# Neighbourhood attention in two steps per block: scores and softmax, then transposes and value products

## The chip, the cores and the metric

The kernel runs on one core of one Trainium2 chip. The metric is the device time in microseconds. A core has a matrix engine (TensorE, PE in the profile; PEld is its loading of stationary operands), a vector engine (VectorE, DVE), an activation engine (ScalarE, ACT), GpSimd (POOL) and SyncE (SP), which here issues the transfers from memory. Each engine works through its own queue in the order in which the kernel was laid out. Matmuls write to PSUM, an accumulator memory that this kernel uses as eight banks of 128 x 512 float32; all other tiles lie in SBUF.

## The reference

A backbone of two layers over 512 latent tokens and 256 context tokens of width 1024, in float32. Every layer has a mixing part, whose three head groups share one input and one output projection, and then a SwiGLU feed-forward part. The mixing part has a gated MLP (A), neighbourhood attention (B) and a bidirectional mLSTM (C). The change concerns B. It has 6 heads of 64 channels; the 512 latent tokens form a grid of 8 rows by 64 columns, and each query sees all 8 rows in a window of 16 columns, clipped at the edges, with a relative bias, and all 256 context tokens:

```python
s_win = jnp.einsum('bhqd,bhqkd->bhqk', q_blk, k_win).astype(jnp.float32) * scale + bias.astype(jnp.float32)
s_ctx = jnp.einsum('bhqd,bhkd->bhqk', q_blk, k_ctx).astype(jnp.float32) * scale
p = jax.nn.softmax(jnp.concatenate([s_win, s_ctx], axis=-1), axis=-1).astype(v.dtype)
return (jnp.einsum('bhqk,bhqkd->bhqd', p[..., :win], v_win)
        + jnp.einsum('bhqk,bhkd->bhqd', p[..., win:], v_ctx))
```

In the first layer the context tokens also attend to the context. The last layer gives no context output.

## The kernel before

Everything is laid out feature by token. A dense product (`dense`, line 137) splits its float32 operands into a high and a low part and makes three matmuls per 128 x 128 weight tile; the weights are loaded by `wload` (line 122) on SP's queue and split by ScalarE (`whi`, line 128) and VectorE (`wlo`, line 129). These products are `dps` in the profile.

The mixing part of a layer is written as Python generators: `do_B(p)` and `do_C(p)` for three pairs of heads each (p = 0, 1, 2), `do_A`, `do_o` (the output gate of C), `do_Cv` (v), `do_Crows` (r), and `do_mods` (m, modulation weights, layer 0 only). A string per layer, `ORDERS[l]` (line 31), says which generator takes its next step and how many, so `B0:3` is three steps of the first head pair. This gives the order in which the code issues instructions. A planner then draws up the queue of each engine from it, when the kernel is built: it takes instructions by their place in that order and by durations that it assumes, so a later instruction that it thinks ready goes ahead of an earlier one that it thinks is not. It also gives tiles their buffers. `after` (line 132) ties one instruction behind another on the same engine. Neither the planner nor its durations are part of the change.

`do_B(p)` (line 483) first makes keys, values and queries of two heads (`bk`, `bv`, `bq`), transposes the values (`bvt`) and loads two bias tiles. Then it goes through attention blocks of 128 queries, one generator step each: three blocks of 16 grid columns each (m = 0, 1, 2) with 256 window keys and 256 context keys; one block of the two edges of the grid, twice 64 queries with 128 window keys each, and 256 context keys; and in layer 0 two blocks of 128 context queries with 256 context keys. That is 18 blocks in layer 0 and 12 in layer 1.

One block is `attend` (line 532). Both heads' scores go to two PSUM tiles (`bsps`). Then for each head in turn: VectorE adds the bias and finds the negated maximum (`nm`), ScalarE takes the exponential and its sum (`prob`, line 564), VectorE inverts the sum and multiplies (line 566), TensorE transposes the probabilities in pieces of 128 x 128 (`ptps`, line 569) and ScalarE copies them to SBUF (`probT`, line 571). Then the value products of both heads run into `bops`, and VectorE copies these to the result `bo`. The PSUM tiles of a block come from the pool `mx`, with four banks, which serves the transposes and products of A, C and the normalisations as well; `dense` takes most of its tiles from the pool `mm`, with three banks. `prob`, `probT` and other working tiles share a pool of seven SBUF buffers, and `bk`, `bv`, `bq`, `bvt` share another seven with the gate, the A group and, afterwards, the residual x, which is loaded back on SP's queue (lines 1056 to 1061).

After the mixing steps the results of A, C and B are split into high and low parts (`put_y`, line 1034) for the output projection.

Of the kernel before, what the change touches and what calls it, by code (L numbers as in the profile page):

```python
# [38 lines left out]
)  # L39
FWD, BWD = [0, 1, 2, 3, 4, 5], [1, 0, 5, 4, 3, 2]  # L40

# [2 lines left out]
def tile_backbone(ctx: ExitStack, tc: tile.TileContext, A, out):  # L44
    nc = tc.nc
    te, ve, ac, gp, sp = nc.tensor, nc.vector, nc.scalar, nc.gpsimd, nc.sync
# [12 lines left out]
    mx = ctx.enter_context(tc.tile_pool(name="mx", bufs=4, space=PSUM))  # L59
# [32 lines left out]
    def pst(pool, name="ps"):  # L92
        return pool.tile([128, 512], F32, tag="ps", name=name)
# [4 lines left out]
    def small(n, name="sm"):  # L98
        return st.tile([128, n], F32, tag="sm%d" % n, name=name)
# [4 lines left out]
    def zat(name, dt=F32):  # L104
        return za.tile([128, 768], dt, tag="z", name=name)
# [208 lines left out]
    for toks in ((2, 3, 4, 5), (0, 1)):  # L314
# [13 lines left out]
        n = len(toks)  # L328
        o = 256 if n == 4 else 0
# [89 lines left out]
    wlast, prev = None, None  # L419
    for k in range(KD):  # L420
# [10 lines left out]
        for stream in (0, 1):  # L431
            prev = norm1_k(0, h_next, x, stream, k)
# [10 lines left out]
    for l in range(2):  # L443
        last = l == 1
# [33 lines left out]
                    te.transpose(out=ps[:, i * 128:(i + 1) * 128], in_=src(c), identity=ident)  # L478
                dst(g, ps)

        bq_t = []

        def do_B(p):
            ku, vu, qu = zat("bk"), zat("bv"), zat("bq")
# [11 lines left out]
            for wi_, (c0, u, is_q) in enumerate(((896, ku, False), (1280, vu, False), (512, qu, True))):  # L496
# [7 lines left out]
                if is_q:  # L504
                    ac.activation(
                        out=u[:, 256:640].rearrange("p (b r i) -> p r b i", b=3, r=8),
                        in_=p3[:, :, 8:56].rearrange("p r (b i) -> p r b i", b=3), func=AF.Copy, scale=sc)
                    for e, cc in enumerate((0, 56)):
                        ve.tensor_scalar(
                            out=u[:, 640 + 64 * e:704 + 64 * e].rearrange("p (r i) -> p r i", r=8),  # L510
                            in0=p3[:, :, cc:cc + 8], scalar1=sc, scalar2=None, op0=ALU.mult)
                else:
                    ac.activation(
                        out=u[:, 256:768].rearrange("p (m r c) -> p r m c", m=4, r=8),
                        in_=p3.rearrange("p r (m c) -> p r m c", m=4), func=AF.Copy)
                if len(parts) > 1:
                    ve.tensor_scalar(out=u[:, 0:256], in0=pp[1], scalar1=sc, scalar2=None, op0=ALU.mult)
            yield
            vt = zat("bvt")
            transposes(  # L520
                lambda g, ps: ac.activation(
                    out=vt[:, g[0] * 128:(g[-1] + 1) * 128], in_=ps[:, 0:len(g) * 128], func=AF.Copy),
                lambda c: vu[:, c * 128:(c + 1) * 128], range(6))
            bias = []
            for j in range(2):
                b = wk.tile([128, 390], F32, tag="bias", name="bias", bufs=2)
                i = sp.dma_start(out=b[:, 0:384], in_=A["bias"][l, 2 * p + j])
# [1 line left out]
                    after(i, start_end)  # L529
                bias.append(b)  # L530

            def attend(q0, segs, L, btile, ops, ocol):
                n = L + 256
                spss = [pst(mx, "bsps") for _ in range(2)]
                jss = [slice(64 * j, 64 * j + 64) for j in range(2)]
                order = [None]

                def chained(*args, **kw):
                    m = te.matmul(*args, **kw)  # L539
                    if order[0] is not None:  # L540
                        after(m, order[0])
                    order[0] = m

                if L == 128:
                    for e in range(2):
                        for sps, js in zip(spss, jss):
                            chained(
                                out=sps[64 * e:64 * e + 64, 0:128], lhsT=qu[js, q0 + 64 * e:q0 + 64 * e + 64],
                                rhs=ku[js, 256 + 384 * e:384 + 384 * e])
                elif L:  # L550
                    for sps, js in zip(spss, jss):
                        chained(
                            out=sps[:, 0:256], lhsT=qu[js, q0:q0 + 128], rhs=ku[js, segs[0] * 128:segs[0] * 128 + 256])
                for sps, js in zip(spss, jss):
                    chained(out=sps[:, L:n], lhsT=qu[js, q0:q0 + 128], rhs=ku[js, 0:256])
                pTs = []
                for j, sps in enumerate(spss):
                    if L:
                        ve.tensor_tensor(out=sps[:, 0:L], in0=sps[:, 0:L], in1=btile[j], op=ALU.add)  # L559
                    nm = small(1, "nm")  # L560
                    ve.tensor_reduce(out=nm, in_=sps[:, 0:n], axis=AX.X, op=ALU.max, negate=True)  # L561
                    pt = wkt("prob")
                    sm_ = small(1, "sum")
                    ac.activation(out=pt[:, 0:n], in_=sps[:, 0:n], func=AF.Exp, bias=nm, accum_out=sm_)  # L564
                    ve.reciprocal(out=sm_, in_=sm_)
                    ve.tensor_scalar(out=pt[:, 0:n], in0=pt[:, 0:n], scalar1=sm_, scalar2=None, op0=ALU.mult)  # L566
                    tps = pst(mx, "ptps")
                    for i in range(n // 128):
                        te.transpose(out=tps[:, i * 128:(i + 1) * 128], in_=pt[:, i * 128:(i + 1) * 128], identity=ident)  # L569
                    pT = wkt("probT")  # L570
                    ac.activation(out=pT[:, 0:n], in_=tps[:, 0:n], func=AF.Copy)
                    pTs.append(pT)
                order[0] = None
                if L == 128:
                    for e in range(2):
                        for i, c in enumerate((2 + 3 * e, 0, 1)):
                            for j, js in ((1, jss[1]), (0, jss[0])):
                                chained(
                                    out=ops[js, ocol + 64 * e:ocol + 64 * e + 64], lhsT=vt[:, c * 128 + 64 * j:c * 128 + 64 * j + 64],
                                    rhs=pTs[j][:, i * 128 + 64 * e:i * 128 + 64 * e + 64], start=(i == 0), stop=(i == 2))  # L580
                else:
                    tl = list(segs) + [0, 1]
                    for i, c in enumerate(tl):
                        for j, js in ((1, jss[1]), (0, jss[0])):
                            chained(
                                out=ops[js, ocol:ocol + 128], lhsT=vt[:, c * 128 + 64 * j:c * 128 + 64 * j + 64],
                                rhs=pTs[j][:, i * 128:(i + 1) * 128], start=(i == 0), stop=(i == len(tl) - 1))

            yield
            res = zct("bo")  # L590
            r3 = res[:, 256:768].rearrange("p (r c) -> p r c", c=64)
            for m in range(3):
                ops = pst(mx, "bops")
                attend(256 + 128 * m, (2 + m, 3 + m), 256, [b[:, 0:256] for b in bias], ops, 0)
                ve.tensor_copy(
                    out=r3[:, :, 8 + 16 * m:24 + 16 * m], in_=ops[:, 0:128].rearrange("p (r i) -> p r i", r=8))
                yield
            ops = pst(mx, "bops")
            attend(640, (), 128, [b[:, 256:384] for b in bias], ops, 0)
            for e, cc in enumerate((0, 56)):  # L600
                ve.tensor_copy(
                    out=r3[:, :, cc:cc + 8], in_=ops[:, 64 * e:64 * e + 64].rearrange("p (r i) -> p r i", r=8))
            yield
            if not last:
                for i in range(2):
                    ops = pst(mx, "bops")
                    attend(128 * i, (), 0, None, ops, 0)
                    ve.tensor_copy(out=res[:, 128 * i:128 * i + 128], in_=ops[:, 0:128])
                    yield
            bq_t.append(res)  # L610

        v65 = [zct("v65").rearrange("p (c h d) -> p c h d", c=2, h=6) for _ in range(3)]
        for t in v65:
# [389 lines left out]
            gens["B%d" % p], gens["C%d" % p] = do_B(p), do_C(p)  # L1003
        for stp in ORDERS[l].split():
            nm, _, cnt = stp.partition(":")
            for _ in range(int(cnt or 99)):
                if next(gens[nm], 0) == 0:
                    break
        for gen in gens.values():
            for _ in gen:  # L1010
                pass
        while fill:
            fill.pop(0)()

# [112 lines left out]
        for pi, (f0, nf) in enumerate(FF_PIECES):  # L1127
# [5 lines left out]
            for fi in range(nf):  # L1133
                f = f0 + fi
# [14 lines left out]
                for pgi, pui, g in zip(pg, pu_, gs):  # L1149
                    o, T = g[1] + (256 if g[0] == "l" else 0), g[2]  # L1150
# [128 lines left out]
```

## Time and profile before

| what | value |
|---|---|
| device time, median of 3 runs | 1732.04 us (1729.26 to 1732.41) |
| the profiled execution's own time | 1729.28 us |
| its span, from first to last instruction | 1726.4 us |
| TensorE busy | 1660.5 us, 96% |
| VectorE busy | 936.3 us, 54% |
| ScalarE busy | 615.3 us, 36% |
| GpSimd busy | 148.2 us, 9% |
| mean granted TensorE clock | 0.984 |

How to read it: the profile is one execution; times in it count from the first instruction. A row of a group gives the line, the engine, the operation, the tile written and the tiles read, then the count, busy time, mean length in ns, and the idle time of the engine directly before, with what ended it. A row of the waits reads "engine tile line <- engine tile line that ended the wait: us in total, times, longest". The granted clock is a share of full speed. Each share is a mean over stages with different limits.

### The profile page before, as it was taken

What the parts mean: (1) busy time and instruction counts of PE and PEld (TensorE: products, weight loads), DVE (VectorE), ACT (ScalarE), POOL (GpSimd) and SP (SyncE); (2) the same over time, 40 slices, a digit from 0 to 9 for tenths busy, and PEclk for the clock granted to TensorE, in tenths of its full rate; (3) what the DMA queues carried; (4) which work ended last, traced back from release to release, by engine and by line L of the source; (5) the groups of instructions that cost most, each with busy time, mean ns of one, the idle gap of its engine ahead of it and who ended that gap; (6) DMA issues with size and microseconds to landing.
All of it is one profiled execution on the core that took longest, in us unless ns stands there. A gap on an engine that the chain in (4) does not pass through costs nothing.

```text
span 1726.4 us, 26247 instructions
## 1 busy us (share of the span) xinstructions
PE 1660.5 (96%) x10784; PEld 1416.0 (82%) x10784; DVE 936.3 (54%) x1697; ACT 615.3 (36%) x1126; POOL 148.2 (9%) x157
## 2 busy tenths in 40 slices
PE   7998999889999999999999999989989999999998
PEld 5886777768888888888888889777869988888888
DVE  4589787635475555344443355585675633333335
ACT  4444344633332211222112244534654522222225
POOL 0000112122200000000000020012033000000000
PEclk9999999979999999999999999989999999999999
DMA  8742313213244434334333233210213322222222
GB/s 290 250 151 70 123 59 102 74 35 102 62 136 132 123 122 135 125 126 128 122 122 104 74 117 105 71 56 28 86 62 117 105 98 98 93 94 94 98 82 95
DMA packets 57143, 184.11 MB, mean 107 GB/s; under 512 B 6720, under 2 KB 8384, under 8 KB 56896
## 3 DMA queue, kind: packets, MB, share of 16 engines
q1 hardware_dynamic: 57024, 182.45, 32.7%
q8 instruction: 84, 1.38, 0.3%
q14 instruction: 35, 0.29, 0.1%
HBM read 175.08 MB, written 7.34 MB: 106 GB/s over the span
## 4 chain that ended last, share of the span: by engine, by line
PE 69%; DVE 5%; ACT 2%; POOL 1%; issue 1%; DVEq 0%; ACTq 0%; POOLq 0%
PE dps L152 60%; PE wps L402 4%; PE vps L627 2%; PE ptps L569 1%; PE nps L876 1%; DVE wlo L129 1%; PE bops L539 1%; ACT pu L862 1%; DVE nm L561 0%; ACT prob L564 0%; DVE prob L566 0%; ACT whi L128 0%; PE bsps L539 0%; DVE bsps L559 0%; PE ups L832 0%
## 5 line engine op out<-in xcount | busy, mean ns | idle before, releaser
L128 ACT ACTIVATE whi<-wraw 128x1024 fp32r<-128x1024 f32 (+2 forms) x224 | 226.6, 1013 | 694.8 <-PE dps L152 429.7
L129 DVE TENSOR_TENSOR wlo<-wraw,whi 128x1024 fp32r<-128x1024 f32 (+2 forms) x224 | 262.5, 1173 | 170.7 <-ACT whi L128 167.9
L152 PE MATMUL dps<-h2lh,wlo 128*128 128x512 f32 (+1 forms) x664 | 258.3, 391 | 0.0
L152 PE MATMUL dps<-h2ll,whi 128*128 128x512 f32 (+1 forms) x664 | 258.3, 391 | 0.0
L152 PE MATMUL dps<-h2lh,whi 128*128 128x512 f32 (+1 forms) x664 | 257.6, 389 | 0.0
L152 PE MATMUL dps<-gh,whi 128*128 128x512 f32 (+1 forms) x576 | 175.2, 341 | 0.0
L152 PE MATMUL dps<-gl,whi 128*128 128x512 f32 (+1 forms) x576 | 175.2, 340 | 0.0
L152 PE MATMUL dps<-gh,wlo 128*128 128x512 f32 (+1 forms) x576 | 175.1, 340 | 0.0
L212 DVE SCALAR_TENSOR_TENSOR wmod<-wmod,c_all 128x1024 f32<-128x1024 f32 x80 | 98.5, 1231 | 98.5 <-DMA wmod<-in_w_mod 97.7
L152 PEld LDWEIGHTS dps<-h2lh,whi 128*128 128x128 f32 x664 | 124.3, 188 | 27.7
L152 PEld LDWEIGHTS dps<-h2lh,wlo 128*128 128x128 f32 x664 | 124.2, 188 | 27.4
L152 PEld LDWEIGHTS dps<-h2ll,whi 128*128 128x128 f32 x664 | 124.3, 188 | 26.7
L1076 DVE SCALAR_TENSOR_TENSOR x<-dps,modT,x 128x512 f32<-128x512 f32 (+1 forms) x112 | 65.3, 596 | 138.0 <-PE dps L152 137.7
L152 PE MATMUL dps<-ll,whi 128*128 128x512 f32 x336 | 136.6, 407 | 1.2 <-DVE ll L109 1.2
L152 PE MATMUL dps<-lh,whi 128*128 128x512 f32 x336 | 134.8, 402 | 1.1 <-ACT whi L128 1.1
L152 PE MATMUL dps<-lh,wlo 128*128 128x512 f32 x336 | 134.7, 401 | 0.0
L152 PEld LDWEIGHTS dps<-gl,whi 128*128 128x128 f32 x576 | 99.3, 188 | 13.5 <-DVE gl L109 0.2
L152 PEld LDWEIGHTS dps<-gh,whi 128*128 128x128 f32 x576 | 99.3, 188 | 13.2
L152 PEld LDWEIGHTS dps<-gh,wlo 128*128 128x128 f32 x576 | 99.3, 188 | 13.2
L212 DVE SCALAR_TENSOR_TENSOR junk<-wmod,c_all 128x1024 f32<-128x1024 f32 x48 | 58.9, 1227 | 76.8 <-DMA wmod<-in_w_mod 76.8
L1153 DVE TENSOR_TENSOR silu<-silu,dps 128x512 f32<-128x512 f32 (+1 forms) x64 | 37.4, 589 | 107.4 <-PE dps L152 107.4
L152 PE MATMUL dps<-h2cl,whi 128*128 128x256 f32 x328 | 92.5, 282 | 0.0
(320 smaller groups left out, 3123.2 us busy)
## 6 DMA issues: line engine op xcount, KB each, us to landing
wmod<-in_w_mod SPq DMA_DIRECT2D x80, 512.0 KB, 3.6
wraw<-in_w_up SPq DMA_DIRECT2D x42, 512.0 KB, 3.2
wraw<-in_w_gate SPq DMA_DIRECT2D x40, 512.0 KB, 3.2
wraw<-in_win_blk SPq DMA_DIRECT2D x34, 512.0 KB, 3.7
wraw<-in_w_down SPq DMA_DIRECT2D x32, 512.0 KB, 3.2
wraw<-in_w_out SPq DMA_DIRECT2D x19, 512.0 KB, 3.3
wraw<-in_w_down SPq DMA_DIRECT2D x21, 384.0 KB, 3.1
wraw<-in_win_cv SPq DMA_DIRECT2D x16, 408.0 KB, 3.2
```

What stands on the lines that cost most here:

```text
L128: ac.activation(out=hi[:, 0:n], in_=raw[:, 0:n], func=AF.Copy)
L129: ve.tensor_tensor(out=lo[:, 0:n], in0=raw[:, 0:n], in1=hi[:, 0:n].bitcast(F32), op=ALU.subtract)
L152: m = te.matmul(out=ps[:, 0:T], lhsT=wt[:, c], rhs=(flo if wh else fhi)(k), start=(k == 0 and wi == 0), stop=(k == nk - 1 and wi == 2),)
L212: ve.scalar_tensor_tensor(out=junk if t < nt - 1 else raw, in0=raw, scalar=1.0, in1=c_all[:, t, :], op0=ALU.mult, op1=ALU.mult, accum_out= ...
L402: m = te.matmul(out=ps[:, 0:T], lhsT=wt[:, cs_], rhs=(flo if wh else fhi)(k), start=(k == 0 and wi == 0), stop=(k == KD - 1 and wi == 2))
L539: m = te.matmul(*args, **kw)
L569: te.transpose(out=tps[:, i * 128:(i + 1) * 128], in_=pt[:, i * 128:(i + 1) * 128], identity=ident)
L627: te.matmul(out=vps[i][:, 0:408], lhsT=tokslice(nm, k, i), rhs=wt[:, cs], start=(k == 0 and wi == 0), stop=(k == KD - 1 and wi == 2))
L862: tabled.append(ac.activation(out=tc_, in_=pc, func=AF.Exp, scale=-1.0, bias=g_))
L876: m = te.matmul(out=banks[j][64 * hf:64 * hf + 64, c * 65:(c + 1) * 65], lhsT=lhsT, rhs=rhs, start=start, stop=stop, skip_group_check=True)
L1076: ve.scalar_tensor_tensor(out=xs, in0=ps, scalar=modT[:, row * 8 + k, g[3]:g[3] + 1], in1=xs, op0=ALU.mult, op1=ALU.add)
L1153: ve.tensor_tensor(out=s, in0=s, in1=pui, op=ALU.mult)
```

## The change

`attend` is cut in two. `scores` makes the score matmuls and the softmax of both heads and returns the two probability tiles; `values` takes the transposes, their copies and the value products. `do_B` issues `scores` of a block, and puts `values` of that block, with the copy of its result, in a list of one entry, `held_b`. The next block, of whichever head pair, empties that list first (`flush_b`) and then issues its own scores. The product tile `bops` is asked for in `values` and no longer ahead of the scores. The transposes of both heads are issued one head after the other with no softmax between them. A new word `f` in the order strings flushes the last block of a layer: in layer 0 ahead of an output gate step (`o:1`), in layer 1 after the last but one step of `C2`. In layer 1 a step `B2:1` is moved ahead of an `o:1`. After the generators `flush_b` is called once more.

```diff
-     "m:1 B2:1 C2:1 m:2 C1:1 o:1 C2:1 o:1 C2:3 o:1 m:1 C2:1"),
+     "m:1 B2:1 C2:1 m:2 C1:1 f:1 o:1 C2:1 o:1 C2:3 o:1 m:1 C2:1"),
...
-     "C2:1 o:1 B1:1 C2:1 C1:1 o:1 C2:1 B2:1 C2:1"),
+     "C2:1 o:1 B1:1 C2:1 C1:1 B2:1 o:1 C2:1 f:1 C2:1"),
...
-        bq_t = []
+        bq_t, held_b = [None] * 3, []
+
+        def flush_b():
+            while held_b:
+                held_b.pop(0)()
...
-            def attend(q0, segs, L, btile, ops, ocol):
+            def scores(q0, segs, L, btile):
                 n = L + 256
                 spss = [pst(mx, "bsps") for _ in range(2)]
...
-                pTs = []
+                pts = []
                 for j, sps in enumerate(spss):
...
                     ve.tensor_scalar(out=pt[:, 0:n], in0=pt[:, 0:n], scalar1=sm_, scalar2=None, op0=ALU.mult)
+                    pts.append(pt)
+                return pts
+
+            def values(pts, segs, L):
+                n = L + 256
+                pTs = []
+                for pt in pts:
                     tps = pst(mx, "ptps")
...
                     pTs.append(pT)
-                order[0] = None
+                ops = pst(mx, "bops")
+                mm_ = chained()
...
-            for m in range(3):
-                ops = pst(mx, "bops")
-                attend(256 + 128 * m, (2 + m, 3 + m), 256, [b[:, 0:256] for b in bias], ops, 0)
-                ve.tensor_copy(
...
+            bq_t[p] = res
+            for q0, segs, L, btile, put in blocks:
+                flush_b()
+                held_b.append(lambda pts=scores(q0, segs, L, btile), segs=segs, L=L, put=put: put(values(pts, segs, L)))
                 yield
...
             nm, _, cnt = stp.partition(":")
+            if nm == "f":
+                flush_b()
+                continue
...
         for gen in gens.values():
             for _ in gen:
                 pass
+        flush_b()
```

More of the change, by code (lines that the diff above doesn't have):

```diff
@@ L530, in do_B, with chained, mm_ @@
                 bias.append(b)
-            def attend(q0, segs, L, btile, ops, ocol):
+            jss = [slice(64 * j, 64 * j + 64) for j in range(2)]
+            def chained():
+                prev = [None]
+                def mm_(*args, **kw):
+                    m = te.matmul(*args, **kw)
+                    if prev[0] is not None:
+                        after(m, prev[0])
+                    prev[0] = m
+                return mm_
+            def scores(q0, segs, L, btile):
                 n = L + 256
                 spss = [pst(mx, "bsps") for _ in range(2)]
[L535 to L542, printed above, removed]
+                mm_ = chained()
                 if L == 128:
@@ L546, in attend @@
                         for sps, js in zip(spss, jss):
-                            chained(
+                            mm_(
                                 out=sps[64 * e:64 * e + 64, 0:128], lhsT=qu[js, q0 + 64 * e:q0 + 64 * e + 64],
@@ L551, in attend @@
                     for sps, js in zip(spss, jss):
-                        chained(
+                        mm_(
                             out=sps[:, 0:256], lhsT=qu[js, q0:q0 + 128], rhs=ku[js, segs[0] * 128:segs[0] * 128 + 256])
                 for sps, js in zip(spss, jss):
-                    chained(out=sps[:, L:n], lhsT=qu[js, q0:q0 + 128], rhs=ku[js, 0:256])
-                pTs = []
+                    mm_(out=sps[:, L:n], lhsT=qu[js, q0:q0 + 128], rhs=ku[js, 0:256])
+                pts = []
                 for j, sps in enumerate(spss):
@@ L572, in attend @@
                     pTs.append(pT)
-                order[0] = None
+                ops = pst(mx, "bops")
+                mm_ = chained()
                 if L == 128:
@@ L576, in attend @@
                         for i, c in enumerate((2 + 3 * e, 0, 1)):
-                            for j, js in ((1, jss[1]), (0, jss[0])):
-                                chained(
-                                    out=ops[js, ocol + 64 * e:ocol + 64 * e + 64], lhsT=vt[:, c * 128 + 64 * j:c * 128 + 64 * j + 64],
+                            for j in (1, 0):
+                                mm_(
+                                    out=ops[jss[j], 64 * e:64 * e + 64], lhsT=vt[:, c * 128 + 64 * j:c * 128 + 64 * j + 64],
                                     rhs=pTs[j][:, i * 128 + 64 * e:i * 128 + 64 * e + 64], start=(i == 0), stop=(i == 2))
@@ L583, in attend @@
                     for i, c in enumerate(tl):
-                        for j, js in ((1, jss[1]), (0, jss[0])):
-                            chained(
-                                out=ops[js, ocol:ocol + 128], lhsT=vt[:, c * 128 + 64 * j:c * 128 + 64 * j + 64],
+                        for j in (1, 0):
+                            mm_(
+                                out=ops[jss[j], 0:128], lhsT=vt[:, c * 128 + 64 * j:c * 128 + 64 * j + 64],
                                 rhs=pTs[j][:, i * 128:(i + 1) * 128], start=(i == 0), stop=(i == len(tl) - 1))
+                return ops
             yield
@@ L591, in do_B, with put_mid, put_edge, put_ctx @@
             r3 = res[:, 256:768].rearrange("p (r c) -> p r c", c=64)
-            for m in range(3):
-                ops = pst(mx, "bops")
-                attend(256 + 128 * m, (2 + m, 3 + m), 256, [b[:, 0:256] for b in bias], ops, 0)
-                ve.tensor_copy(
+            def put_mid(m):
+                return lambda ops: ve.tensor_copy(
                     out=r3[:, :, 8 + 16 * m:24 + 16 * m], in_=ops[:, 0:128].rearrange("p (r i) -> p r i", r=8))
-                yield
[L598 to L610, printed above, removed]
+            def put_edge(ops):
+                for e, cc in enumerate((0, 56)):
+                    ve.tensor_copy(
+                        out=r3[:, :, cc:cc + 8], in_=ops[:, 64 * e:64 * e + 64].rearrange("p (r i) -> p r i", r=8))
+            def put_ctx(i):
+                return lambda ops: ve.tensor_copy(out=res[:, 128 * i:128 * i + 128], in_=ops[:, 0:128])
+            blocks = [(256 + 128 * m, (2 + m, 3 + m), 256, [b[:, 0:256] for b in bias], put_mid(m)) for m in range(3)]
+            blocks.append((640, (), 128, [b[:, 256:384] for b in bias], put_edge))
+            if not last:
+                blocks += [(128 * i, (), 0, None, put_ctx(i)) for i in range(2)]
+            bq_t[p] = res
+            for q0, segs, L, btile, put in blocks:
+                flush_b()
+                held_b.append(lambda pts=scores(q0, segs, L, btile), segs=segs, L=L, put=put: put(values(pts, segs, L)))
+                yield
         v65 = [zct("v65").rearrange("p (c h d) -> p c h d", c=2, h=6) for _ in range(3)]
```

## Prediction

> **What bounds the kernel now.** I read the page first (busy shares and the chain that ended last), then the busy time by stage, then TensorE's waits by stage, and last the queues of the engines in order of time around the worst of these waits. From the page:
>
> ```profile
> span 1726.4 us, 26247 instructions
> ...
> PE 1660.5 (96%) x10784; PEld 1416.0 (82%) x10784; DVE 936.3 (54%) x1697; ACT 615.3 (36%) x1126; POOL 148.2 (9%) x157
> ...
> PE dps L152 60%; PE wps L402 4%; PE vps L627 2%; PE ptps L569 1%; PE nps L876 1%; DVE wlo L129 1%; PE bops L539 1%; ACT pu L862 1%; DVE nm L561 0%; ACT prob L564 0%; DVE prob L566 0%; ACT whi L128 0%; PE bsps L539 0%; DVE bsps L559 0%; PE ups L832 0%
> ```
>
> TensorE is busy for 1660.5 of 1726.4 us, and the chain is mostly its dense products (dps). The change takes no work from it, so it can gain only where TensorE stands still or runs at a lower clock. The next view gives busy time per engine in three stretches, with the granted clock behind it: the mixing part of layer 0, the dense products of both layers between, the mixing part of layer 1.
>
> ```profile
> core 0: us, PE busy (x) PEld busy (x) DVE busy (x) ACT busy (x) POOL busy (x), PEclk, DMA share, GB/s
> ...
> 56.00:407.00 351.00, 317.76 (x2600) 263.97 (x2599) 253.39 (x542) 161.62 (x353) 54.89 (x54) 0.96 0.31 101
> 407.00:1050.00 643.00, 642.68 (x3681) 561.23 (x3679) 315.93 (x487) 164.65 (x254) 31.35 (x27) 1.00 0.37 116
> 1050.00:1309.00 259.00, 242.34 (x1968) 200.67 (x1967) 164.77 (x364) 126.85 (x264) 46.45 (x52) 0.97 0.21 66
> ```
>
> The middle stretch has nothing to give (0.3 us idle). The mixing parts idle for 351.0 - 317.8 = 33.2 us and 259.0 - 242.3 = 16.7 us, 49.9 us together. That is the ceiling, clock aside. The waits of TensorE (what waited for what: us, times, longest) say how much of it is attention; layer 0 in three pieces, 100 to 166, 166 to 338 and 338 to 362 us:
>
> ```profile
> PE ptps L569 <- DVE prob L566: 6.8, 2, 4.9
> ...
> PE ptps L569 <- DVE mla L706: 0.4, 1, 0.4
> ```
>
> ```profile
> PE ptps L569 <- DVE prob L566: 3.3, 6, 1.0
> ```
>
> ```profile
> PE ptps L569 <- DVE prob L566: 7.8, 4, 2.3
> PE bops L539 <- ACT probT L571: 1.1, 2, 0.6
> PE dps L152 <- ACT og L997: 0.7, 1, 0.7
> ```
>
> and layer 1, 1050 to 1309 us:
>
> ```profile
> PE ptps L569 <- DVE prob L566: 6.1, 10, 1.4
> ...
> PE ptps L569 <- DVE var L967: 1.5, 1, 1.5
> ```
>
> These are 7.2, 3.3, 9.6 and 7.6 us, **27.7 us** of the 49.9. All but 1.8 of them are transposes (ptps) that stand at the head of TensorE's queue before the probabilities are normalised, with other ready matmuls queued behind them. The rest (22.2 us) waits for the mLSTM chain, for projections and for x, which the change does not touch.
>
> **Why a block waits.** The second-last attention block of layer 0, on TensorE, ScalarE and VectorE in order of time (start, length, instruction, idle time before it):
>
> ```profile
> 346.37 2.81 PE L876 MATMUL nps<-v,pu 128*64 128x65 f32 x48
> ...
> 349.12 1.08 PE L876 MATMUL nps<-cs,qw 64*64 64x65 f32 x40
> ...
> 350.12 0.70 PE L539 MATMUL bsps<-bk,bq 64*128 64x256 f32 x4
> ...
> 351.38 0.47 ACT L564 ACTIVATE prob<-bsps,nm 128x256 f32<-128x256 f32 x1 [0.88 <-DVE nm L561]
> ...
> 353.15 0.66 PE L569 MATMUL ptps<-cst,prob 128*128 128x128 f32 x2 [2.32 <-DVE prob L566]
> 353.84 0.38 ACT L571 ACTIVATE probT<-ptps 128x256 f32<-128x256 f32 x1 [1.90 <-PE ptps L569]
> 354.12 0.47 ACT L564 ACTIVATE prob<-bsps,nm 128x256 f32<-128x256 f32 x1
> ...
> 355.41 0.66 PE L569 MATMUL ptps<-cst,prob 128*128 128x128 f32 x2 [1.60 <-DVE prob L566]
> 356.11 0.38 ACT L571 ACTIVATE probT<-ptps 128x256 f32<-128x256 f32 x1 [1.43 <-PE ptps L569]
> 356.54 1.12 PE L539 MATMUL bops<-probT,bvt 128*64 128x128 f32 x8 [0.47 <-ACT probT L571]
> 357.60 1.23 PE L539 MATMUL bsps<-bk,bq 64*128 64x256 f32 x4
> ```
>
> Two things hold it up. ScalarE's queue is in order and runs exponential, copy, exponential, copy: the second head's exponential (354.12) stands behind the first head's copy (353.84), and that copy behind the first head's transposes. And the next block's scores (357.60) start only behind the products of this one. TensorE stands for 2.32 + 1.60 + 0.47 = 4.4 us within one block, though the 2.8 and 1.1 us of mLSTM output products just ahead of it were ready work that could have stood inside it.
>
> **The change, part by part.** No instruction is added or taken away: the same scores, additions, maxima, exponentials, transposes, copies and value products, the same two bias loads per pass. So no engine's busy time changes, and each term is a wait that goes or comes. What moves per block is 4 to 8 transposes, two ScalarE copies, 8 to 24 value products and one or two VectorE copies. They go behind whatever the schedule names between two blocks, or directly ahead of the next scores. They issue no transfer and nothing on GpSimd, so SP's and POOL's queues are passed by nothing. On ScalarE both exponentials of a block now precede both copies. On VectorE only the copy of the result moves, past a few other short instructions.
>
> *The waits of 27.7 us.* Of 30 blocks, 23 have other steps between them and the next block or flush; 7 are followed directly by the next one (4 in layer 0, 3 in layer 1), where only the next block's scores can fill the gap. What comes late next in each stretch sets how much is kept:
>
> - 338 to 362 us, 9.6 us: mLSTM products before it and the third gate projection behind it can fill it, and the two heads' chains now overlap. I take two thirds, 6.4.
> - 100 to 166 us, 7.2 us: here VectorE itself is nearly full (44.93 of 50 us, first row of the next fence). Weights (wlo) and evictions for the matmuls that should fill the gap come from the same queue. I take half, 3.6.
> - 166 to 338 us, 3.3 us: scattered, short, with projections around them. Two thirds, 2.2.
> - Layer 1, 7.6 us: no modulation steps as filler and 3 direct pairs among 12 blocks. Half, 3.8.
>
> Together 16.0 us; the bounds are a third of 27.7, 9.2, and all of it. The transposes have their wait in one row over the whole run (last numbers), which bounds this from a second side:
>
> ```profile
> L569 PE MATMUL ptps<-cst,prob 128*128 128x128 f32 x204 | 34.7, 287 | 27.0 <-DVE prob L566 24.1 <-DVE var L967 1.5 <-DVE mla L706 0.4
> ```
>
> *The clock.* The granted clock (the column behind the busy times) falls after the two worst places:
>
> ```profile
> 120.00:170.00 50.00, 41.30 (x280) 32.75 (x279) 44.93 (x107) 22.21 (x47) 3.78 (x5) 0.97 0.27 86
> ...
> 340.00:360.00 20.00, 11.23 (x140) 8.28 (x141) 5.61 (x22) 5.06 (x18) 2.03 (x2) 0.66 0.00 1
> 360.00:380.00 20.00, 17.91 (x161) 15.98 (x161) 7.55 (x18) 9.19 (x26) 6.73 (x9) 0.83 0.20 68
> ```
>
> What TensorE lost by it is busy time times the missing share: 0.03 x 41.3 = 1.2, 0.34 x 11.23 = 3.8, 0.17 x 17.91 = 3.0, together 8.1 us. If the waits shrink, part of the dips goes; none to all of it, and I take half, 4.0. [...]
>
> *What is given back.* TensorE arrives earlier at everything behind, and VectorE, busy 253.4 of 351.0 us in layer 0, does not get faster; some of the gain becomes waits for evictions, x and the mLSTM chain. No row prices that; the bounds are none and all, and since VectorE's share there is nearer to three quarters than to one, I take a third of 20.0, 6.7 us.
>
> *The tail.* The last block's products are flushed by hand: in layer 0 ahead of an output-gate projection, in layer 1 behind the last mLSTM output products. The transposed values of the pass (bvt, one of seven such buffers) stay until then, and the loads of x into these buffers wait for free ones:
>
> ```profile
> 1288.96 0.86 SPq L1059 DMA_DIRECT2D x<-xd  x2
> ...
> 1302.16 9.28 SPq L1059 DMA_DIRECT2D x<-xd  x6
> ```
>
> Six of eight go out between 1302 and 1311 us already now, when the buffers of the gate come free, so the one buffer that comes later costs nothing if the flush is over by 1311 us: the gate's own buffers cover it. Without that cover it is one load that goes out late, by less than the 9.3 us that the six now take. Swapping B2 with the gate in layer 1's schedule moves nothing: that B2 step only ends its generator.
>
> The sum: -16.0 - 4.0 + 6.7 = **-13.3 us**. The profiled execution took 1729.28 us (span 1726.4), almost the lowest of the runs shown (1729.26); the median is 2.8 us above it. So 1716.0 in that execution's terms, **1718.7 us** at the median, a ratio of 0.992. With the bounds of the terms the forecast's own range is 1704 to 1727 us.
>
> **The rivals.**
>
> *All of it comes.* The stalls go wholly and the clock stays up: 27.7 + 8.1 = 35.8 us, 1696 us. For it: the waits are one mechanism. Against: 7 direct pairs and the full VectorE.
>
> *It is hidden anyway.* The order on each engine is drawn up by the planner from the order of the code and its own durations; it already moves scores and projections about. If it puts the transposes where it thinks the probabilities are ready, they wait as before, or the wait passes to the mLSTM chain. Against it: the copy between the exponentials must go. The time: 1731 us.
>
> *The banks.* The four PSUM banks of the mx pool become the bound, and the kernel gets slower. Before, a block needs one bank for products, two for scores and one or two in turn for transposes. Now a values step wants three (two transposes, one product) while the next scores hold two: five of four. If the scores are placed first, the second transposes wait until the next block's exponentials have freed a bank:
>
> ```profile
> L559 DVE TENSOR_TENSOR bsps<-bsps,bias 128x256 f32<-128x256 f32 x36 | 13.7, 425 | 2.3 <-PE bsps L539 2.2
> ...
> L561 DVE TENSOR_REDUCE nm<-bsps 128x1 f32<-128x512 f32 x36 | 23.9, 681 | 0.0
> ...
> L564 ACT ACTIVATE prob<-bsps,nm 128x512 f32<-128x512 f32 x36 | 24.7, 686 | 28.5 <-DVE nm L561 28.5
> L564 ACT ACTIVATION_READ_ACCUMULATOR prob<-bsps,nm 128x1 f32 x60 | 11.9, 198 | 0.0
> ```
>
> That is 2 x (0.425 + 0.681) + 0.686 + 0.198 = 3.1 us per boundary, 87 us over the 28 boundaries (17 and 11) before cover. Today TensorE sees 27.0 / 30 = 0.9 us of the 4.4 us of a bare block, so a fifth shows: 17.4 us. Against the gain of 13.3 that is +4.1, 1736 us. It decides from 13.3 / 87, 15% uncovered. For it: mx also serves the mLSTM chain. Against: the values stand ahead of the scores in the code, and two score banks fall free soon after.
>
> **How the numbers follow.** Forecast 0.50, all of it 0.10, hidden 0.18, banks 0.18; 0.04 stays for a planner's order that is worse in another way. A measurement here tells from no change about 0.2%, 3.5 us. Faster: 0.50 + 0.10 and a little of "hidden", 0.62; same 0.16; slower 0.22. The range 1704 to 1737 leaves out most of the case "all of it" and half of the slower ones.
>
> **What would show it.** Right: TensorE's waits for prob fall from 24.1 to below 10 us; both exponentials of a block stand side by side on ScalarE; the next scores start before a block's products; the clock between the last blocks of layer 0 stays above 0.9; the mixing stretches shorten by about 11 us (two thirds of 12.2 + 4.0) and 2.5 us (two thirds of 3.8). Wrong: transposes still wait for prob, or wait for ScalarE's copies or exponentials (banks); idle time of the same size on sps, ups or dps; VectorE's share unchanged while its queue holds the evictions.

## The result and the profile after

The changed kernel takes 1714.55 us (median of 6 runs, 1712.27 to 1721.28), the kernel before 1728.18 us (median of 6 runs of both sessions, 1726.33 to 1732.41). The ratio is **0.9925, 95% interval 0.9908 to 0.9941**, so 13 us faster. The forecast was 1718.7 us and a ratio of 0.992. The size is as forecast; the experiments below show that the reason given for it was only half right.

The page of the changed kernel, span and busy time of the engines:

```profile
span 1713.5 us, 26246 instructions
...
PE 1654.2 (97%) x10784; PEld 1413.0 (82%) x10784; DVE 940.7 (55%) x1697; ACT 609.2 (36%) x1123; POOL 154.9 (9%) x157
```

TensorE has the same 10784 matmuls and 6.3 us less busy time. To see where 12.9 us of span went, both traces are cut at the first value projection of the mLSTM (vps), at the start of the long run of output products, at the first such projection of layer 1, and at the start of its run of output products. Busy time by stage, before:

```profile
65.08:407.45 342.37, 309.93 (x2555) 257.74 (x2554) 248.73 (x529) 155.06 (x345) 54.89 (x54) 0.96 0.31 98
```

```profile
407.45:1058.50 651.05, 650.73 (x3727) 568.38 (x3727) 316.75 (x490) 165.92 (x257) 31.35 (x27) 1.00 0.36 115
1058.50:1308.98 250.48, 233.82 (x1917) 193.05 (x1916) 163.47 (x361) 125.29 (x261) 46.45 (x52) 0.97 0.21 66
```

and after:

```profile
63.20:393.15 329.95, 305.32 (x2555) 254.77 (x2554) 251.82 (x529) 154.29 (x345) 58.13 (x54) 0.97 0.32 102
```

```profile
393.15:1045.79 652.64, 652.32 (x3728) 568.62 (x3727) 316.48 (x490) 165.81 (x257) 31.37 (x27) 1.00 0.36 115
1045.79:1296.04 250.25, 233.77 (x1919) 194.91 (x1917) 165.30 (x361) 119.92 (x258) 49.08 (x52) 0.97 0.21 66
```

Layer 0's mixing part is shorter by 342.4 - 330.0 = **12.4 us**, with the same 2555 matmuls in it: 7.8 us less idle time of TensorE (32.4 to 24.6) and 4.6 us less busy time, while the granted clock went from 0.96 to 0.97. Layer 1's mixing part gave 0.2 us. Its last mLSTM transposes end 1.7 us sooner after the cut (248.8 us, 250.5 before), but the run of output products then starts 1.4 us behind them, with this wait:

```profile
1296.04 0.39 PE L152 MATMUL dps<-yAl,whi 128*128 128x256 f32 x1 [1.07 <-DVE yAl L109]
```

The first projection came 1.9 us earlier. That does not belong to the change: the matmuls ahead of it stand in the same order in every trace of this case, and it began late, at 65.1 us or after, in just the four traces whose granted clock fell on the way to it (0.91 to 0.94 over the first 56 us, 1.00 in the other ten). The first 56 us, before and after, with the granted clock in the third last column:

```profile
0.00:56.00 56.00, 46.84 (x326) 34.71 (x327) 29.49 (x70) 26.21 (x50) 1.79 (x12) 0.94 0.82 283
```

```profile
0.00:56.00 56.00, 45.53 (x337) 34.25 (x338) 30.73 (x74) 26.59 (x50) 1.79 (x12) 1.00 0.82 292
```

The dense stretch between took 1.6 us longer, with the same matmuls in it; why was not taken apart. It is no scatter of single traces: kernels for which the planner drew the same queues (below) repeat this stretch within 0.02 us.

TensorE's waits (what waited for what: us, times, longest) after, first in layer 0 and then in layer 1:

```profile
PE ptps L584 <- DVE prob L574: 12.4, 10, 7.5
...
PE ptps L584 <- DVE rden L922: 1.6, 1, 1.6
```

```profile
PE sps L823 <- DVE cq L792: 7.7, 2, 5.9
PE tokps L755 <- ACT rA L735: 2.2, 1, 2.2
PE bops L542 <- ACT probT L586: 2.0, 1, 2.0
PE rowps L680 <- ACT rI L681: 1.3, 1, 1.3
...
PE ptps L584 <- DVE prob L574: 0.3, 2, 0.2
```

and in layer 1 before:

```profile
PE sps L803 <- DVE cq L772: 5.2, 2, 3.4
...
PE tokps L735 <- ACT rA L715: 1.4, 1, 1.4
```

In layer 1 the waits of attention fell from 7.6 to 2.3 us, and the mLSTM chain took nearly all of it back: cq from 5.2 to 7.7, rA from 1.4 to 2.2, and rI, 1.3, is new. In layer 0 the transposes still wait 14.2 us, over half of it in one place, with the engine that it waits for ahead of it (start, length, instruction):

```profile
149.84 0.98 DVE L715 TENSOR_TENSOR_SCAN rM<-rI,mst 6x128 f32<-6x128 f32 x2
150.85 0.16 DVE L573 RECIPROCAL sum<-sum 128x1 f32<-128x1 f32 x1
...
151.29 0.35 DVE L574 TENSOR_SCALAR prob<-prob,sum 128x256 f32<-128x256 f32 x1
```

```profile
151.80 0.45 PE L584 MATMUL ptps<-cst,prob 128*128 128x128 f32 x1 [7.49 <-DVE prob L574]
```

That is the stretch in which VectorE is full (busy for 45.95 of the 50 us from 120 to 170 us); its running maxima (rM) stand between the steps of the softmax, and the wait grew from 4.9 to 7.5 us.

The second-last attention block of layer 0 now, on ScalarE and then on TensorE:

```profile
327.57 0.47 ACT L572 ACTIVATE prob<-bsps,nm 128x256 f32<-128x256 f32 x1 [2.15 <-DVE nm L569]
...
328.03 1.05 ACT L128 ACTIVATE whi<-wraw 128x1024 fp32r<-128x1024 f32 x1
328.98 0.46 ACT L572 ACTIVATE prob<-bsps,nm 128x256 f32<-128x256 f32 x1
...
330.64 0.39 ACT L586 ACTIVATE probT<-ptps 128x256 f32<-128x256 f32 x1
```

```profile
329.21 0.38 PE L584 MATMUL ptps<-cst,prob 128*128 128x128 f32 x2
...
330.95 0.41 PE L584 MATMUL ptps<-cst,prob 128*128 128x128 f32 x2 [0.31 <-DVE prob L574]
...
335.40 0.66 PE L542 MATMUL bops<-probT,bvt 128*64 128x128 f32 x8
```

The second exponential no longer stands behind a copy, only behind a weight split (whi), and TensorE stands for 0.3 us in the block and no longer for 4.4. How long an exponential is held shows when it is set against its maximum (nm), which VectorE finishes ahead of it. The second head's maximum in this block, first before and then after (here both heads' in one row):

```profile
352.13 0.41 DVE L561 TENSOR_REDUCE nm<-bsps 128x1 f32<-128x256 f32 x1
```

```profile
327.05 0.76 DVE L569 TENSOR_REDUCE nm<-bsps 128x1 f32<-128x256 f32 x2 [0.26 <-PE bsps L542]
```

Before, it was ready at 352.54 us, and the exponential began at 354.12, 1.6 us later, although ScalarE was idle for 1.90 us ahead of the copy. Over all 30 blocks the second head's exponential began 2.5 us after its maximum on average, the first head's 0.5 us; in the changed kernel it is 0.5 and 0.4 us. ScalarE's own waits for transposes, over the whole run, before and after:

```profile
ACT probT L571 <- PE ptps L569: 76.4, 44, 4.6
```

```profile
ACT probT L586 <- PE ptps L584: 18.4, 28, 2.3
```

### The profile page after: what moved, and what is told of

Same layout as the page of the kernel before. It is cut to its first block, busy times and chain, and to the rows that moved or that the text cites. A ratio compares the mean times of both kernels' runs of the same rounds, so it can differ in the third digit from the quotient of the medians.

```text
span 1713.5 us, 26246 instructions
## 1 busy us (share of the span) xinstructions
PE 1654.2 (97%) x10784; PEld 1413.0 (82%) x10784; DVE 940.7 (55%) x1697; ACT 609.2 (36%) x1123; POOL 154.9 (9%) x157
## 4 chain that ended last, share of the span: by engine, by line
PE 79%; DVE 10%; issue 3%; ACT 3%; DMA 2%; POOL 1%; SPq 0%; DVEq 0%; ACTq 0%; POOLq 0%
PE dps L152 63%; PE wps L402 5%; PE vps L647 3%; DMA wmod<-in_w_mod 1%; DVE wlo L129 1%; PE bops L542 1%; PE ptps L584 1%; PE bsps L542 1%; DVE nm L569 1%; PE nps L896 1%; DVE junk L212 1%; DVE rM L715 1%; DVE rF L706 1%; ACT pu L882 1%; ACT prob L572 1%
## 5 line engine op out<-in xcount | busy, mean ns | idle before, releaser
L152 PEld LDWEIGHTS dps<-h2lh,wlo 128*128 128x128 f32 x664 | 124.3, 188 | 28.4
```

The lines of the kernel that those rows point to most:

```text
L152: m = te.matmul(out=ps[:, 0:T], lhsT=wt[:, c], rhs=(flo if wh else fhi)(k), start=(k == 0 and wi == 0), stop=(k == nk - 1 and wi == 2),)
```

## The experiments

Theory 1 is the one of the forecast: the gain comes from the other steps that stand between the two halves of a block. Theory 2: it comes from taking the two heads together inside a block, or from asking for the product bank later. Theory 3: any redraw of the planner's order moves the time by such an amount. All ratios are against the kernel before, with 95% intervals.

**Cut in two, nothing put off.** The values step runs right behind its scores, in both layers.

```diff
                 flush_b()
                 held_b.append(lambda pts=scores(q0, segs, L, btile), ...)
+                if True:
+                    flush_b()
                 yield
```

> The block is cut in two as in the change, but the values step follows its scores at once, with nothing between them: both heads' softmax, then both heads' transposes and products. Theory 1 (the gain of 13.6 us comes from the other steps that stand between the two halves): little of it is left, ratio to the kernel before 0.997 to 1.001, 1723 to 1730 us. Theory 2 (the gain comes from pairing the two heads, exponential beside exponential, and from asking for the product bank later): all of it is there, ratio about 0.992, 1714 us. Theory 3 (any redraw of the planner's order moves the time by some 10 us either way): anything from 0.992 to 1.008.

Measured: 1712.21 us, ratio 0.9903 (0.9878 to 0.9928). **All of the gain is there with nothing put off. Theory 1 falls.** No other steps have to be laid out between the halves in the code. Nor is the gain a matter of TensorE's waits alone: its transposes still wait 19.8 us in this trace, against 26.0 in the kernel before; in layer 0's mixing part TensorE idles 3.6 us less and is busy 5.6 us less, at a granted clock of 0.98 against 0.96.

**Put off in one layer only.** The same extra flush, under `if l == 1` and under `if l == 0`.

> The values step is put off in layer 0 alone; in layer 1 it follows its scores at once. The profiles say that layer 0's mixing stretch gave 14.3 us and layer 1's 0.3. If that holds by itself and not by luck of the two traces, the ratio to the kernel before is 0.992 to 0.994, 1714 to 1718 us. If layer 1 gained something that the two traces hide, 0.995 or above, 1720 us and more.

Measured: 1713.17 us, 0.9906 (0.9884 to 0.9927). Just below what was expected (0.992 to 0.994), and it no longer says anything on putting off, since the next kernel is as fast.

> The values step is put off in layer 1 alone; in layer 0 it follows its scores at once. Theory 1: layer 1 is held by the mLSTM chain (TensorE's wait for cq grew from 5.2 to 7.7 us there), so what is left is at most what pairing the heads gives in layer 0: ratio 0.997 to 1.001, 1723 to 1730 us, and the same time as the kernel with nothing put off within 3 us. Theory 2: as fast as the change.

Measured: 1712.74 us, 0.9904 (0.9883 to 0.9925). The expectation of theory 1 missed by over 10 us.

**Scores first.** The next block's scores are issued ahead of the held values step.

```diff
-                flush_b()
-                held_b.append(lambda pts=scores(q0, segs, L, btile), ...)
+                nxt = (lambda pts=scores(q0, segs, L, btile), ...)
+                flush_b()
+                held_b.append(nxt)
```

> As the change, but the next block's scores are issued ahead of the held values step and no longer behind it, so that scores stand first in the code and the values step, which wants three banks of the pool, finds two of four taken. Theory 1 (banks do not decide, the planner moves scores and values by readiness): within 3 us of the change, 1712 to 1718 us. The rival of the banks: waits of transposes for ScalarE or for exponentials, 3.1 us per boundary before cover, a fifth of 87 us showing: about 17 us slower than the change, 1731 us.

Measured: 1715.34 us, 0.9916 (0.9898 to 0.9935), as fast as the change. The rival of the banks falls with it. The order did change: TensorE's wait moved from the transposes to the copies, with this row at the head of its waits:

```profile
PE bops L542 <- ACT probT L586: 11.3, 15, 4.2
```

That left theory 2 in its two halves, and theory 3.

**The late bank alone**, on the kernel before: `ops = pst(mx, "bops")` moved behind both heads' softmax and transposes.

```diff
+                ops = pst(mx, "bops")
                 if L == 128:
                     for e in range(2):
                         for i, c in enumerate((2 + 3 * e, 0, 1)):
```

> The kernel before, with one edit: the bank for the value products is asked for after both heads' softmax and transposes, no longer ahead of the scores. Heads are still taken one after the other. If the late bank is the cause of the 13 to 16 us (a fifth claim on the four banks of mx that holds other work up), ratio 0.990 to 0.994; if pairing the heads is, 0.997 to 1.002.

Measured: 1727.43 us, 1.000 (0.999 to 1.001). The bank is not it: in this trace and in that of the kernel before, the same instructions stand in the same order on TensorE, VectorE, ScalarE and GpSimd.

**The pairing with the early bank**: the block cut in two, nothing put off, and the product bank asked for at the start of `scores`.

> As the kernel with the block cut in two and nothing put off, but the bank for the products is asked for ahead of the scores, as before. If pairing the two heads is the cause, 0.990 to 0.994 (1711 to 1718 us); if the late bank is, 0.997 to 1.002.

Measured: 1713.24 us, 0.9923 (0.9900 to 0.9947). The gain stays with the pairing. Here too the bank changed no order: on these four engines the instructions stand as in the first experiment.

**The copies alone.** On the kernel before; each head's transposes stay behind its own softmax, and only the two copies on ScalarE move behind both.

```diff
-                pTs = []
+                pTs, tpss = [], []
...
+                    tpss.append(tps)
+                for tps in tpss:
                     pT = wkt("probT")
                     ac.activation(out=pT[:, 0:n], in_=tps[:, 0:n], func=AF.Copy)
```

> The kernel before, with one edit: the two copies of the transposed probabilities are issued after both heads' softmax and transposes, so that the second head's exponential no longer has a copy ahead of it in the code; each head's transposes still stand right behind its own softmax. If the in-order queue of ScalarE is what pairing takes away (its waits for transposes were 76.4 us before and 39.3 us with the heads paired), all or most of the gain is here: 0.990 to 0.995. If what matters is where the transposes stand in TensorE's order, 0.997 to 1.002.

Measured: 1718.51 us, 0.9943 (0.9925 to 0.9961). Inside what was expected of ScalarE's queue. The traces say more: from this edit the planner draws the queues of the first experiment. In this kernel, in the block cut in two and in the same with the early bank, the same instructions stand in the same order on TensorE, VectorE, ScalarE and GpSimd (the traces leave out the numbers of buffers). So moving two copies in the code does all that the pairing does, and 1718.51, 1712.21 and 1713.24 us are three measurements of one order; their spread of 6 us is wider than their intervals would suggest. The run also says less than was hoped: TensorE's order was redrawn along with ScalarE's, so it does not tell the one from the other.

This trace began 4.5 us later than that of the first experiment (first projection at 67.1 and 62.6 us), with a granted clock of 0.91 against 1.00 over the first 56 us. From there on layer 0's mixing part is as short. But the same order splits differently into idle and busy time, with the clock, first in this kernel, then with the block cut in two:

```profile
67.10:400.77 333.67, 309.55 (x2555) 257.08 (x2554) 251.33 (x529) 157.78 (x347) 56.96 (x54) 0.96 0.31 101
```

```profile
62.60:395.76 333.16, 304.32 (x2555) 253.02 (x2554) 251.41 (x529) 157.67 (x347) 55.82 (x54) 0.98 0.32 101
```

**Two controls for luck.** The second head ahead of the first, in the kernel before and in the changed one. In the code only the order of the heads changes, in the changed kernel for the transposes too.

```diff
-                for j, sps in enumerate(spss):
+                for j, sps in ((1, spss[1]), (0, spss[0])):
...
```

> A control for the planner's luck: the kernel before with the second head's softmax, transposes and copy taken first, nothing else. The amount of work, waits and banks is the same. If the order that the planner draws up is a lottery of some 10 us, this may land anywhere from 0.992 to 1.008; if the 13 us belong to the structure, it stays within 0.3% of the kernel before, 1723 to 1733 us.

Measured: 1730.13 us, 1.0007 (0.9995 to 1.0019).

> The changed kernel with the second head's softmax and transposes ahead of the first head's, the counterpart of the same control on the kernel before. The planner redraws its order, ScalarE's queue stays exponential, exponential, copy, copy. If the gain belongs to that order: 0.989 to 0.995, 1709 to 1720 us. If it is luck of one drawing, it may be lost, up to 1.0.

Measured: 1714.40 us, 0.9915 (0.9900 to 0.9930). A redraw of each kernel stays where its structure is. Theory 3 falls, as far as one redraw of each can show.

**The maxima first.** On the kernel before: both heads' bias additions and maxima ahead of the first exponential. ScalarE's queue stays exponential, copy, exponential, copy.

```diff
+                nms = []
                 for j, sps in enumerate(spss):
                     if L:
                         ve.tensor_tensor(out=sps[:, 0:L], in0=sps[:, 0:L], in1=btile[j], op=ALU.add)
                     nm = small(1, "nm")
                     ve.tensor_reduce(out=nm, in_=sps[:, 0:n], axis=AX.X, op=ALU.max, negate=True)
+                    nms.append(nm)
+                for j, sps in enumerate(spss):
+                    nm = nms[j]
                     pt = wkt("prob")
```

> The kernel before, with the second head's bias addition and maximum issued ahead of the first head's exponential. So both heads' scores are ready for ScalarE early, but its queue still runs exponential, copy, exponential, copy, as laid out. New theory (the first head's copy, which waits for the first head's transposes, holds up the second head's exponential in ScalarE's in-order queue): no gain, 0.997 to 1.002, 1722 to 1731 us. If pairing helps by VectorE's order or by the earlier maxima, 0.990 to 0.995.

Measured: 1743.06 us, **1.0083** (1.0066 to 1.0100). Not only no gain: 14 us slower, so the expected 0.997 to 1.002 was missed on the slow side. The earlier maxima buy nothing, because the second exponential still goes behind the first copy. In this block its maximum was ready at 351.12 us, and it began at 352.83:

```profile
350.56 0.56 DVE L562 TENSOR_REDUCE nm<-bsps 128x1 f32<-128x384 f32 x1
```

```profile
352.44 0.49 ACT L575 ACTIVATE probT<-ptps 128x384 f32<-128x384 f32 x1 [1.35 <-PE ptps L573]
352.83 0.58 ACT L568 ACTIVATE prob<-bsps,nm 128x384 f32<-128x384 f32 x1
```

ScalarE's waits for transposes are the longest of all:

```profile
ACT probT L575 <- PE ptps L573: 90.4, 46, 5.3
```

Why it is slower than before, and not the same, was not taken apart.

**Without the flush words.** The changed kernel with the order strings of before.

> The changed kernel with the order strings of before: no flush by hand, so the last block's products come after all generators. If the flush points matter, 2 to 4 us slower than the change (1717 to 1719 us), since the last products stand behind the last mLSTM steps; if not, within 2 us of it.

Measured: 1713.88 us, 0.9909 (0.9893 to 0.9925), as fast as the change. The flush points do not matter.

**Stage by stage.** Cut in two, nothing put off, and the softmax in three loops over the heads: additions and maxima, exponentials, scalings.

```diff
...
                     ve.tensor_reduce(out=nm, in_=sps[:, 0:n], axis=AX.X, op=ALU.max, negate=True)
+                    nms.append(nm)
+                for sps, nm in zip(spss, nms):
                     pt = wkt("prob")
                     sm_ = small(1, "sum")
                     ac.activation(out=pt[:, 0:n], in_=sps[:, 0:n], func=AF.Exp, bias=nm, accum_out=sm_)
+                    pts.append(pt)
+                    sums.append(sm_)
+                for pt, sm_ in zip(pts, sums):
                     ve.reciprocal(out=sm_, in_=sm_)
                     ve.tensor_scalar(out=pt[:, 0:n], in0=pt[:, 0:n], scalar1=sm_, scalar2=None, op0=ALU.mult)
-                    pts.append(pt)
...
```

> The block cut in two with nothing put off, and the softmax of the two heads taken stage by stage: both additions and maxima, both exponentials, both scalings. If ScalarE's order is all that counts, the same as the block cut in two with each head's softmax in one piece, 0.988 to 0.993 (1708 to 1716 us); if the earlier exponential helps beyond that, below 0.988.

Measured: **1707.35 us, 0.9874** (0.9854 to 0.9895). It beats the kernel before by 22 us and the change too, whose interval (0.9908 to 0.9941) lies apart. Layer 0's mixing part is the shortest of all, with the least busy time for its 2555 matmuls and the highest granted clock, 0.99:

```profile
65.40:389.35 323.95, 300.09 (x2555) 251.15 (x2554) 250.65 (x529) 155.22 (x345) 58.81 (x54) 0.99 0.32 104
```

The ratio lies just below the mark set beforehand, 0.988, but its interval reaches beyond that mark. Against the block cut in two with each head's softmax in one piece (0.9878 to 0.9928) the intervals overlap, and three measurements of that order spread by 6 us, so what the stages add to the pairing is not settled.

Put side by side, one trace each, the kernels fall into two groups by the order that ScalarE's queue has in all 30 blocks (E exponential, C copy; with the scores first, exponentials of the next block may come in too). The third column is the mean time from the end of the second head's maximum to the start of its exponential:

| kernel | ScalarE | second exponential after its maximum, us | layer 0 mixing, us | TensorE idle in it, us | ratio |
|---|---|---|---|---|---|
| before | E C E C | 2.5 | 342.4 | 32.4 | 1 |
| late bank | E C E C | 2.5 | 343.0 | 32.0 | 1.000 |
| before, heads swapped | E C E C | 2.9 | 345.6 | 29.1 | 1.0007 |
| maxima first | E C E C | 3.4 | 353.9 | 38.1 | 1.0083 |
| copies last | E E C C | 0.6 | 333.7 | 24.1 | 0.9943 |
| cut in two, nothing put off | E E C C | 0.6 | 333.2 | 28.8 | 0.9903 |
| the same, early bank | E E C C | 0.5 | 329.7 | 24.7 | 0.9923 |
| the change | E E C C | 0.5 | 330.0 | 24.6 | 0.9925 |
| the change, heads swapped | E E C C | 0.8 | 330.7 | 19.2 | 0.9915 |
| scores first | copies behind both E | 0.5 | 331.0 | 28.4 | 0.9916 |
| stage by stage | E E C C | 0.7 | 324.0 | 23.9 | 0.9874 |

The eleven rows are eight orders, since the first two have the same queues and the first three of E E C C have, too. The three kernels that are not in the table (put off in one layer, and without the flush words) have E E C C as well, and 327.0 to 331.5 us. Within one order layer 0's mixing part differs by up to 4.0 us; the two groups are 8.7 us apart. ScalarE's waits for transposes are 75.6 to 90.4 us in the first group and 41.6 us or less in the second. TensorE's idle time is not to be compared for the swapped kernels, where it counts more busy time for the same value products (24.6 and 24.0 us in this stage, 17.7 and 16.6 unswapped).

## Why the prediction was right, and where it was wrong

**The size was right.** 1718.7 us was forecast, 1714.55 measured; 0.992 and 0.9925. The places were right in part: layer 0 was to give about 11 us and gave 12.4, layer 1 2.5 and gave 0.2. Since the waits were priced by the wrong reason, as the next paragraphs show, so close a fit is partly luck. The forecast's own range of 1704 to 1727 us does not come out of the bounds of its terms; with all of them at their ends, these give 1696 to 1732 us.

**The mechanism was half right.** The prediction named two things that hold a block up: ScalarE's in-order queue with the copy between the exponentials, and the next scores behind this block's products. It then priced neither by itself. It priced the waits of the transposes by how many steps stand between the two halves ("Of 30 blocks, 23 have other steps between them"). **That is the step that failed.** With no steps between, the whole gain stays (0.9903 and 0.9923); without the flush words too (0.9909). What was left aside as a side effect, "On ScalarE both exponentials of a block now precede both copies", is what has to be there for the gain: moving the two copies alone makes the planner draw the very queues of the cut block, and keeping the copy between the exponentials, with everything ahead of it earlier, gains nothing. ScalarE's queue, served in order in these traces, with a wait in the middle of one head's chain turned two parallel chains into one serial chain: the second exponential began 2.5 us after its maximum on average, and in the changed kernel 0.5 us.

That ScalarE's queue is served in order shows in the kernel with the maxima first: the second exponential was ready at 351.12 us, ScalarE idled for 1.35 us ahead of the copy (352.44), and the exponential started behind it (352.83).

**The terms of the sum, in layer 0 and layer 1.**

- *Waits.* 16.0 us of 27.7 were to go. The transposes and products waited 16.5 us after (14.2 and 2.3), so 11.2 went. In the last stretch the forecast of two thirds, 3.2 us left of 9.6, was about good: 4.2 us of transposes' waits are left in the whole stretch from 300 to 393 us. Where VectorE is full, half of 7.2 was to go, and none did: one wait of 7.5 us stands there. In layer 1 half of 7.6 was to go, and 5.3 did.
- *The clock.* 4.0 us forecast; 4.6 us less busy time for the same matmuls. That is one pair of traces. Three traces of one order have 304.3, 305.0 and 309.6 us of busy time for them, so this term is not fixed by the order.
- *Given back.* A third was taken everywhere. In layer 1 nearly all of it was given back, to the mLSTM chain (4.6 of 5.3 us); in layer 0 none shows. The kernels that put nothing off (cut in two, early bank, copies last) did give the 2.5 us in layer 1: 247.9 to 248.0 us against 250.5. The two errors, too much removed and too much given back, offset each other by luck.
- *The tail.* Costs nothing, as said: without the flush words the time is the same.

**The rivals.** "All of it comes" did not, but the kernel with the softmax by stages came to 1707 us. "Hidden anyway" and "banks" are excluded, the second by the kernel that issues the scores first, which was to cost 17 us and cost nothing that can be measured.

**The marks set beforehand.** Waits for prob below 10 us: 12.7, missed. Exponentials side by side: no copy stands between them any more, but a weight split of 1.05 us does in the block shown. Clock above 0.9 between the last blocks of layer 0: not quite, it still fell to 0.83 in one slice of 10 us (340 to 350 us), but no longer to 0.66 for 20 us. The next scores ahead of a block's products: no, they still stand behind them (products at 335.40, scores at 335.99), and so it is on TensorE in all 30 blocks, so putting off the values overlapped no neighbouring blocks there.

What stays open: whether the copy between the exponentials hurts by the second head's chain alone, by the weight splits that stand behind it in ScalarE's queue, or by the order that the planner then draws for TensorE; no run separates them.

## What to carry to other kernels

When two independent chains run through the same engines, look in each engine's queue for an instruction of one chain that waits, ahead of a ready instruction of the other (here ScalarE's copy: the second exponential began 2.5 us after its maximum on average, and 0.6 us with the copies behind both). Issue the two chains stage by stage, so that waiting instructions come last. Price that queue by itself, before any rearrangement of whole blocks; here moving two copies did the work for which a deferred step with flush points was built. A forecast of the right size is no proof of its reason: leave the presumed cause out and see whether the gain goes.

## What the runs showed of the hardware

In one place the clock fell after a wait of 2.1 us. In the changed kernel's trace the granted clock is 0.51 in this slice, after 1.00 in the 10 us before it; the only wait of TensorE from 230 to 262 us is this one, which ends as the slice begins:

```profile
250.00:260.00 10.00, 9.74 (x56) 7.68 (x57) 6.17 (x14) 2.99 (x8) 4.67 (x5) 0.51 0.33 105
```

```profile
PE sps L823 <- DVE rden L922: 2.1, 1, 2.1
```

So part of the difference between two traces can lie in the clock: in layer 0's mixing part 4.6 us of busy time, at 0.97 against 0.96, beside 7.8 us of idle time. But the clock differs between executions of one order, too. The first 56 us, with the matmuls in the same order, had a granted clock of 1.00, 0.94 or 0.91, and layer 0's mixing part took 329.7, 333.2 and 333.7 us in three traces of one order. The dense stretch, at a granted clock of 1.00, took 650.65, 650.67 and 650.67 us in the same three; over all kernels it took 648.3 to 653.1 us. A stage should be compared from a common event, an edit's queues with those of the other kernels before its time is read as its own, and a gain of 0.3% needs repeated runs.
